# Prompt's value tiles, attention from the third plain tile, operand loads beside plain tiles, ordered taps, fp32 branches

## The chip, the cores and the metric

One core of one Trainium2 chip runs the whole program in one launch. The metric is device time in microseconds (us); the time before is the median of three runs.

## The reference, cut to what matters

One encoder layer is applied with the same weights to a prompt group (512 tokens) and a sample group (1024 tokens). The model width is 1024 and the FFN width 2816, all in fp32.

```python
def token_mixer(h, ...):                       # h = rms_norm(x, norm1_g)
    z = h @ w_in                               # 1024 -> 6400 columns
    br_a = conformer_conv(z[..., OFF_A:OFF_B]) # GLU, depthwise conv of 31 taps, LayerNorm, SiLU, @ w_out_a
    br_b = multiscale_pool(z[..., OFF_B:OFF_C])
    br_c = short_gated_conv(z[..., OFF_C:OFF_D])
    q, k, v = jnp.split(z[..., OFF_D:OFF_G], 3, axis=-1)
    br_d = neighbourhood_attention(q, k, v, rpb) @ w_out_d
    gates = jax.nn.sigmoid(z[..., OFF_G:].reshape(b, t, 4, 1024) + b_gate)
    merged = gates[:, :, 0] * br_a + gates[:, :, 1] * br_b + gates[:, :, 2] * br_c + gates[:, :, 3] * br_d
    return merged @ w_o
...
x = x + token_mixer(rms_norm(x, norm1_g), ...)
x = x + conv_glu_ffn(rms_norm(x, norm2_g), w_up, ffn_conv_w, w_down)
return rms_norm(x, final_g)
```

## The kernel before

The 1536 tokens stand in the columns, in three chunks of 512 (chunk 0 is the prompt, 1 and 2 the sample); the 1024 features are eight blocks `k` of 128 partitions. An fp32 product is made of three matmuls on a high and a low part of each operand (`mm3`, lines 121 to 125: high by high, high by low, low by high). `split` (line 113) makes the two parts: a copy on ScalarE and a subtraction on VectorE. All transfers are issued from one queue, SyncE's (`SP.dma_start`). The kernel is written in a framework that places semaphores itself and fixes each engine's order of instructions ahead of the run: a planner takes, among the instructions that its model holds ready, the one written first. `tc.high_priority()` lets a block go ahead of that; `keep_in_program_order` pins an instruction behind the one that was written just before it on its engine.

The stages that the change touches, in order:

- **Row sums, queries, keys, values** (lines 320 to 509). For chunk 0 the four tiles `z0` (two of queries, two of keys) are made of un-normalized x (`raw0`), for chunks 1 and 2 of normalized h. `stats` (384) squares x on ScalarE and adds on GpSimd and VectorE; `scale` (395) turns the sums into a factor per token with 16 one-column matmuls and some twelve small VectorE steps (`rms_scale`, 138), and writes it on a diagonal `dg`; `spread` (154) sends it over all partitions by one matmul; `norm` (401) multiplies x by it and splits. `qk_out` (406) writes q and k to DRAM. `value_tile` (468) makes the values of 128 tokens with 24 matmuls of 256 columns and writes them by 8 small transfers; it runs for chunks 1, 2, 0, all three on normalized h, after the queries and keys. Beside chunk 1's value tiles chunk 0 is normalized (line 505), beside chunk 2's `operands` (487) writes the pair operands T1 to T4 to DRAM.
- **Plain tiles and attention** (517 to 759). Twelve tiles of 128 output features over three chunks (`ftile`, 24 matmuls for each chunk) feed the conformer, pooling and short-conv branches. Attention has 24 steps; `start` (630) loads q and k of a pair of heads, and `pump(STEPS)` writes 0.7 of a step for each chunk of a plain tile. Attention of the first pair of heads is started ahead of the first plain tile. Branch results are split and both parts go to DRAM (`branch`, `spill`).
- **Gate stage** (764 to 922). The 32 gate tiles are made in 16 pairs; chunks 1 and 2 by a scheme of seven products `y`, `wz`, `xz` on combined operands and combined weights (`PairWeights`, 230), chunk 0 by two plain tiles. `side` (789) is a second stream of work, written between the products by `tick`: 62 taps of the 31-tap conv (2 on ScalarE, 60 on VectorE, line 804) and then the LayerNorm and SiLU. With TAPS = 6, six of its pieces are written for each pair.
- **Merge** (931 to 956). Gates are read back (`g`, 1 MB each), the branches are projected and multiplied by the gates. `load_bs` (855) reads the branch parts from DRAM.

After that come the projection with `w_o` and the FFN, which the change leaves as they are.

## Time and profile before

| | |
|---|---|
| median of 3 runs | 2310.15 us (2308.76 to 2310.45) |
| profiled execution | 2310.91 us, its span 2309.1 us |
| TensorE busy | 2213.5 us, 96% of the span |
| VectorE, ScalarE, GpSimd busy | 1332.6, 771.9, 612.3 us |
| mean granted TensorE clock | 0.975 of full speed |
| DMA | 269.63 MB, mean 117 GB/s |

Busy times are those of one execution under the hardware profiler. A granted clock of 1.00 stands for 2.4 GHz and 0.50 for 1.2 GHz. A row of a window gives its bounds, its length, then busy us and instructions of TensorE's matmuls, its weight loads, VectorE, ScalarE and GpSimd, then the granted clock, the DMA share and GB/s. In the views a line is that of the helper that records the instruction, so the tile names tell the stages apart: `zt` and `z0` queries and keys, `zv` values, `z` plain tiles, `s`, `tp`, `o` attention, `yg`, `wg`, `xg`, `ppg` gates, `y` merge.

### The profile page before, as it was taken

Reading aid. Unit: us, or ns where it says so; the run is one execution under the profiler, and the core shown is the slowest. Engines: PE = TensorE matmul, PEld = TensorE weight load, DVE = VectorE, ACT = ScalarE, POOL = GpSimd, SP = SyncE. Lnnn points to the kernel's source line nnn. Section 1 sums busy time; section 2 is a strip of 40 time slices with the busy share of each in tenths; the row PEclk is TensorE's granted clock in tenths of the full one; section 3 lists DMA queues with packets and bytes.
Section 4 is the critical chain, followed back from the end, with each engine's and each line's share of the span. In section 5 each row is a group of like instructions: output and inputs, shape, how many; then the busy total and the mean of one; then the engine's idle time right before and its main releaser. Section 6 shows DMA issues by size and latency. Waiting matters only on the chain.

```text
span 2309.1 us, 27008 instructions
## 1 busy us (share of the span) xinstructions
PE 2213.5 (96%) x9898; PEld 1797.7 (78%) x9898; DVE 1332.6 (58%) x1946; ACT 771.9 (33%) x1322; POOL 612.3 (27%) x695
## 2 busy tenths in 40 slices
PE   6896999999999999989999999999999999999997
PEld 4794767767788878868787788888888888888886
DVE  4742374588932234167618898788887775441414
ACT  4322544433233335200313443333333333321112
POOL 2111322223211112044224444444444440000001
PEclk8897999999999999999999999999999999999998
DMA  5265251363132223776342321111111114532231
GB/s 208 88 226 173 92 176 67 105 226 119 58 122 86 80 85 141 256 282 226 129 128 93 136 74 64 64 56 63 65 60 64 64 60 153 189 107 70 69 97 51
DMA packets 121205, 269.63 MB, mean 117 GB/s; under 512 B 13808, under 2 KB 24560, under 8 KB 118000
## 3 DMA queue, kind: packets, MB, share of 16 engines
q1 hardware_dynamic: 121072, 267.90, 34.3%
q8 instruction: 78, 1.28, 0.2%
q14 instruction: 55, 0.45, 0.1%
HBM read 173.73 MB, written 94.12 MB: 116 GB/s over the span
## 4 chain that ended last, share of the span: by engine, by line
PE 48%; DVE 2%; issue 0%; POOL 0%; DMA 0%; ACT 0%; POOLq 0%; SPq 0%; DVEq 0%; ACTq 0%
PE yp L124 5%; PE yp L125 5%; PE yp L123 5%; PE ppu L123 3%; PE ppu L125 3%; PE ppu L124 3%; PE o L124 2%; PE o L125 2%; PE o L123 2%; PE p3T L124 1%; PE p3T L123 1%; PE p3T L125 1%; PE p2T L125 1%; PE p2T L124 1%; PE p1T L124 1%; PE p1T L125 1%
## 5 line engine op out<-in xcount | busy, mean ns | idle before, releaser
L123 PE MATMUL yp<-fs,wdhi 128*128 128x512 f32 x480 | 187.0, 391 | 0.0
L124 PE MATMUL yp<-fs,wdhi 128*128 128x512 f32 x480 | 186.9, 389 | 0.0
L125 PE MATMUL yp<-fs,wdlo 128*128 128x512 f32 x480 | 186.8, 389 | 0.0
L1140 POOL TENSOR_TENSOR u<-u,u 128x512 f32<-128x512 f32 x63 | 97.3, 1544 | 194.5 <-DVE u L1133 131.2
L115 DVE TENSOR_TENSOR fs<-fr,fs 128x512 fp32r<-128x512 f32 x63 | 43.5, 690 | 181.5 <-ACT fs L114 181.5
L804 DVE SCALAR_TENSOR_TENSOR acc<-glu,pt,acc 128x1552 f32<-128x1552 f32 x60 | 122.2, 2036 | 12.9 <-ACT acc L802 11.9
L123 PE MATMUL z<-hh,wh_i 128*128 128x512 f32 x288 | 118.4, 411 | 0.2 <-ACT wh_i L114 0.2
L124 PE MATMUL z<-hl,wh_i 128*128 128x512 f32 x288 | 116.4, 404 | 0.0
L125 PE MATMUL z<-hh,wl_i 128*128 128x512 f32 x288 | 115.7, 402 | 0.0
L114 ACT CAST fs<-fr 128x512 fp32r<-128x512 f32 x63 | 39.1, 621 | 198.6 <-DMA fr<-f_d 100.8
L123 PEld LDWEIGHTS yp<-fs,wdhi 128*128 128x128 f32 x480 | 90.1, 188 | 19.4 <-issue 0.5
L124 PEld LDWEIGHTS yp<-fs,wdhi 128*128 128x128 f32 x480 | 90.1, 188 | 19.4 <-issue 0.5
L592 POOL TENSOR_TENSOR bm<-R,pt 128x384 f32<-128x384 f32 (+1 forms) x48 | 44.7, 936 | 228.0 <-DVE mx L599 164.1
L1233 POOL TENSOR_TENSOR x<-x,rs 128x256 f32<-128x256 f32 x11 | 7.6, 730 | 367.0 <-DVE acc L1221 363.3
L125 PEld LDWEIGHTS yp<-fs,wdlo 128*128 128x128 f32 x480 | 90.1, 188 | 18.6
L1133 DVE SCALAR_TENSOR_TENSOR u<-c,pt,u 128x512 f32<-128x512 f32 x88 | 100.4, 1179 | 0.0
L1132 DVE SCALAR_TENSOR_TENSOR u<-c,pt,u 128x512 f32<-128x512 f32 x88 | 86.9, 1025 | 0.0
L123 PE MATMUL y<-bh,wh_wo 128*128 128x512 f32 x192 | 75.6, 394 | 10.0 <-DVE g L942 10.0
L1139 ACT ACTIVATE u<-u 128x512 f32<-128x512 f32 x66 | 41.8, 633 | 112.4 <-DVE u L1133 112.3
L942 DVE TENSOR_TENSOR g<-y,g 128x512 f32<-128x512 f32 x96 | 62.1, 682 | 27.1 <-DMA g<-gate_d 18.8
L124 PE MATMUL o<-ml,wh_o 128*128 128x512 f32 x192 | 75.1, 391 | 1.4 <-DVE ml L115 1.4
L124 PE MATMUL y<-bl,wh_wo 128*128 128x512 f32 x192 | 75.4, 393 | 0.0
(497 smaller groups left out, 6420.9 us busy)
## 6 DMA issues: line engine op xcount, KB each, us to landing
g<-gate_d SPq DMA_DIRECT2D x24, 1024.0 KB, 5.3
wr_u<-in_w_up SPq DMA_DIRECT2D x44, 512.0 KB, 3.5
f_d<-u SPq DMA_DIRECT2D x66, 256.0 KB, 2.0
fr<-f_d SPq DMA_DIRECT2D x66, 256.0 KB, 2.6
wr_g<-in_w_in SPq DMA_DIRECT2D x32, 512.0 KB, 4.0
wdr<-in_w_dn SPq DMA_DIRECT2D x23, 512.0 KB, 3.6
gate_d<-gp SPq DMA_DIRECT2D x32, 256.0 KB, 4.1
x<-in_xT SPq DMA_DIRECT2D x24, 256.0 KB, 5.7
```

What stands on the lines that cost most here:

```text
L114: S.copy(hi, src)
L115: V.tensor_tensor(lo, src, hi.bitcast(F32), ALU.subtract)
L123: PE.matmul(ps, w[0][:, ws], x[0], start=first, stop=False, **kw)
L124: PE.matmul(ps, w[0][:, ws], x[1], start=False, stop=False, **kw)
L125: PE.matmul(ps, w[1][:, ws], x[0], start=False, stop=last, **kw)
L592: G.tensor_tensor(bmv, rv, cm[:, None, :].broadcast_to([P, nk, 32]), ALU.add)
L804: V.scalar_tensor_tensor(a, g, w, a, ALU.mult, ALU.add)
L942: V.tensor_tensor(g[:, i], z, g[:, i], ALU.mult)
L1132: V.scalar_tensor_tensor(b, r[:, 0:C], pc("fc", f * 3), b, ALU.mult, ALU.add)
L1133: V.scalar_tensor_tensor(b, r[:, 2 : C + 2], pc("fc", f * 3 + 2), b, ALU.mult, ALU.add)
L1139: S.activation(ug, ug, AF.Silu)
L1140: (V if j == NJ - 1 else G).tensor_tensor(uv, uv, ug, ALU.mult)
```

## The change

- Order of loads at the start: the remaining query weights, half of chunk 1 of x, the remaining key weights, the parameters, the rest of chunk 1, the value weights, chunk 2. Chunk 1 is squared first, then chunk 0.
- The prompt's four value tiles are made of un-normalized x right after the four `z0` tiles, and scaled by the row factor as they leave PSUM. The first two `norm` of chunk 1 and `qk_out` of chunk 0 are written between them, all `norm` steps with high priority. Chunk 0 of x is loaded a second time beside chunk 2's value tiles and normalized there, each first step pinned.
- Plain tiles take the chunks in the order 1, 2, 0. Two plain tiles are written ahead of attention; STEPS is 0.95. Attention's buffers lie in a group of their own, which is closed once its last step is written and two plain tiles are left. The pair operands are loaded from then on.
- Each VectorE tap is pinned in program order; five pieces of `side` are written for each gate pair.
- Branch results go to DRAM as one fp32 tile and are split after they are read back.
- Pools are placed on two sides of the memory; the tiles for big rows in the plain stage fall from 8 to 3.

```diff
-STEPS = 0.7
-TAPS = 6
+STEPS = 0.95
+TAPS = 5
...
-    bs_d = {(i, k, c): dram(f"bs_d{i}{k}{c}", [2, P, C]) for i in range(4) for k in range(2) for c in range(NC)}
+    bs_d = {(i, k, c): dram(f"bs_d{i}{k}{c}", [P, C]) for i in range(4) for k in range(2) for c in range(NC)}
...
-        def spill(i, k, c, hi, lo):
-            for t, m in ((hi, 0), (lo, 1)):
-                SP.dma_start(bs_d[i, k, c][m], t.bitcast(F32))
+        pairs = [(gates[2 * n], gates[2 * n + 1]) for n in range(16)]
+
+        def keep(ins):
+            return tc.keep_in_program_order(ins)
+
+        tp = None
+
+        def tt(name, dt=F32):
+            return tp.tile([P, C], dt, tag="t", name=name)
...
-            SP.dma_start(pt, par[:, NG:])
-            for k in range(KT):
-                load_x(k, 1)
+            def square(k, c):
+                q = tt(f"sq0_{c}{k}")
+                S.activation(q, x[k, c], AF.Square)
+                if k in (0, 4):
+                    sq[c, k] = q
+                else:
+                    a = sq[c, k & 4]
+                    (V if c == 1 and k > 4 else G).tensor_tensor(a, a, q, ALU.add)
+
+            more_w(0, 13, HD**-0.5)
+            for k in range(4):
+                load_x(k, 1)
+            more_w(1, 15, None)
+            SP.dma_start(pt, par[:, NG:])
+            for k in range(4, KT):
+                load_x(k, 1)
+            for k in range(KT):
+                square(k, 1)
+            vw = [[tt(f"vw{m}{a}", F32R) for a in range(4)] for m in "hl"]
+            for t in range(2):
+                raw = wp.tile([P, DM], F32, tag="wraw", name=f"wr_v{t}")
+                SP.dma_start(raw, w_in[16 + t])
+                for a in range(4):
+                    hi, lo = (vw[m][a].rearrange("p (k t d) -> p k t d", k=2, t=2)[:, :, t, :] for m in range(2))
+                    split(hi, lo, raw[:, a * 256 : (a + 1) * 256].rearrange("p (k d) -> p k d", k=2))
+            for k in range(KT):
+                square(k, 0)
...
             def scale(c):
                 ps = ztile(f"rb0_{c}")
                 dg = tt(f"dg0_{c}")
-                rms_scale(dg, ps, stat[c], DM)
-                stat[c] = dg, ps
+                y = rms_scale(dg, ps, [sq[c, 0], sq[c, 4]], DM)
+                stat[c] = dg, ps, y
 
...
                 z0[n] = ztile(f"zt0{n}")
                 for k in range(KT):
                     w, ws = quad_w(n, k)
                     mm3(z0[n], w, ws, raw0[k], k == 0, k == KT - 1)
-                    if n == 1 and k == 2:
+                    if n == 3 and k == 5:
+                        scale(1)
+                    if n == 3 and k == 6:
                         scale(0)
-                    if n == 1 and k == KT - 1:
-                        spread(*stat[0])
-                        rbp = tt("rbp")
-                        S.copy(rbp, stat[0][1])
-                    if n == 3 and k == 3:
-                        scale(1)
...
-                    split(hi, lo, raw[:, a * 256 : (a + 1) * 256].rearrange("p (k d) -> p k d", k=2))
-
-            def value_tile(c, b):
+
+            def value_tile(c, b, hc, ys=None):
                 z = ztile(f"zv{c}{b}")[:, :256]
                 for k in range(KT):
-                    xh, xl = (y[:, cols(b)] for y in h[c][k])
+                    xh, xl = (y[:, cols(b)] for y in hc[k])
...
-                split(oo[:, :, 0], oo[:, :, 1], z.rearrange("t (p d) -> t p d", p=2))
+                zz = z.rearrange("t (p d) -> t p d", p=2)
+                if ys is None:
+                    split(oo[:, :, 0], oo[:, :, 1], zz)
+                else:
+                    split_scaled(oo[:, :, 0], oo[:, :, 1], zz, ys[:, b : b + 1])
...
+            for b in range(4):
+                value_tile(0, b, raw0, stat[0][2])
+                if b == 1:
+                    spread(*stat[1][:2])
+                    spread(*stat[0][:2])
+                    rbp = tt("rbp")
+                    S.copy(rbp, stat[0][1])
+                if b > 1:
+                    with tc.high_priority():
+                        norm(b - 2, 1)
+                    for n in (2 * b - 4, 2 * b - 3):
+                        qk_out(*QUAD[n], 0, z0[n])
+            for c in (1, 2):
+                zz = [ztile(f"zt{c}{n}") for n in range(4)]
+                for k in range(KT):
+                    if c == 2 or k > 1:
+                        with tc.high_priority():
+                            norm(k, c)
+                    for n in range(4):
+                        w, ws = quad_w(n, k)
+                        mm3(zz[n], w, ws, h[c][k], k == 0, k == KT - 1)
+                    if c == 1:
+                        square(k, 2)
+                    if c == 1 and k == 7:
+                        scale(2)
+                if c == 1:
+                    spread(*stat[2][:2])
+                for n in range(4):
+                    qk_out(*QUAD[n], c, zz[n])
...
-            for c in (1, 2, 0):
+            for c in (1, 2):
                 for b in range(4):
-                    value_tile(c, b)
+                    value_tile(c, b, h[c])
                     if c == 1:
+                        operands(b)
+                    else:
                         for k in (2 * b, 2 * b + 1):
-                            V.scalar_tensor_tensor(x[k, 0], x[k, 0], pc("g1", k), rbp, ALU.mult, ALU.mult)
+                            load_x(k, 0)
+                            keep(V.scalar_tensor_tensor(x[k, 0], x[k, 0], pc("g1", k), rbp, ALU.mult, ALU.mult))
                             h[0][k] = pr[k] = hl(f"hh{k}_0"), hl(f"hl{k}_0")
                             split(*h[0][k], x[k, 0])
-                    if c == 2:
-                        operands(b)
-
...
-                gop = pool(p1, "gop", 7)
-                ap = pool(p1, "ap", 2)
-                kp = pool(p1, "kp", 2)
+                bigp = pool(p1, "bigp", 3, side="right")
+                gop = pool(p1, "gop", 5, side="right")
+                att = p1.enter_context(ExitStack())
+                ap = pool(att, "ap", 2)
+                kp = pool(att, "kp", 2)
+                qp = pool(att, "qp", 4)
...
-                            branch(3, p, qc, ot[:, ch(qc)])
+                            SP.dma_start(bs_d[3, p, qc], ot)
 
                     def start():
                         for n in "qk":
                             for m in "hl":
-                                pl_, tag = (bigp, "big") if n == "q" else (kp, "k")
-                                t[n + m] = pl_.tile([P, PADW], F32R, tag=tag, name=f"{n}{m}{p}")
-                                SP.dma_start(t[n + m][:, :T].bitcast(F32), qk_d[n, p, m])
+                                t[n + m] = (qp if n == "q" else kp).tile([P, T], F32R, tag=n, name=f"{n}{m}{p}")
+                                SP.dma_start(t[n + m].bitcast(F32), qk_d[n, p, m])
...
+                            o = go(f"ob{i}{c}")
+                            S.activation(o, m, AF.Copy, scale=pc("ps", i))
+                            SP.dma_start(bs_d[1, i, c], o)
...
-                        branch(2, i, c, o)
+                        SP.dma_start(bs_d[2, i, c], o)
...
+                def operand_loads():
+                    nonlocal tp
+                    att.close()
+                    tp = pool(tstack, "tpb", TPN)
+                    for n in ("T2", "T3", "T1", "T4"):
+                        for k in range(4):
+                            ops[n, k] = tt(f"{n}gh{k}", F32R), tt(f"{n}gl{k}", F32R)
+                            for m in range(2):
+                                SP.dma_start(ops[n, k][m].bitcast(F32), t_d[n, k][m])
+
+                cb = [conv_branch(i) for i in range(2)]
+                sh = [short_branch(i) for i in range(2)]
+                cb[0][0]()
+                cb[0][1]()
                 attention_pair(0)
-                conv_branch(0)
-                conv_branch(1)
+                cb[1][0]()
                 pool_branch(0)
+                cb[1][1]()
                 pool_branch(1)
                 attention_pair(1)
-                sh = [short_branch(i) for i in range(2)]
                 sh[0][0]()
+                sh[0][1]()
                 sh[1][0]()
-                sh[0][1]()
+                sh[0][2]()
                 sh[1][1]()
+                sh[1][2]()
 
...
+                wg = PairWeights("g", lambda n: tuple(w_in[gate_idx(*g)] for g in pairs[n]), lambda name: tt(name))
-                    for c in range(NC):
+                    left -= 1
+                    for c in (1, 2, 0):
...
                         pump(STEPS)
-                while bg:
-                    bg.pop(0)()
+                        if left < 3 and not bg and tp is None:
+                            operand_loads()
+                assert tp is not None
...
-            tp = pool(phb, "tpb", TPN)
-            go1 = pool(phb, "gob", 8)
+            cvp = pool(phb, "cvp", 2, side="right")
+            go1 = pool(phb, "gob", 8, side="right")
...
-            for n in ("T2", "T3", "T1", "T4"):
-                for k in range(4):
-                    ops[n, k] = tt(f"{n}gh{k}", F32R), tt(f"{n}gl{k}", F32R)
-                    for m in range(2):
-                        SP.dma_start(ops[n, k][m].bitcast(F32), t_d[n, k][m])
...
-                            V.scalar_tensor_tensor(a, g, w, a, ALU.mult, ALU.add)
+                            keep(V.scalar_tensor_tensor(a, g, w, a, ALU.mult, ALU.add))
...
-                        hi, lo = go(f"ch{i}{c}", F32R), go(f"cl{i}{c}", F32R)
-                        split(hi, lo, a)
-                        spill(0, i, c, hi, lo)
+                        SP.dma_start(bs_d[0, i, c], a)
...
+                        t = go(f"bs{i}{k}{c}")
+                        SP.dma_start(t, bs_d[i, k, c])
                         bs[i, k, c] = hl(f"bh{i}{k}{c}"), hl(f"bl{i}{k}{c}")
-                        for m in range(2):
-                            SP.dma_start(bs[i, k, c][m].bitcast(F32), bs_d[i, k, c][m])
+                        split(*bs[i, k, c], t)
```

## Rows read from the trace of the kernel before

**Rows 1.** Windows (start:end, length, busy by engine with counts, clock, DMA), the opening.
```profile
0.00:46.00 46.00, 34.88 (x130) 26.47 (x130) 16.77 (x38) 21.40 (x37) 11.62 (x13) 0.89 0.62 215
46.00:61.10 15.10, 2.08 (x2) 0.50 (x2) 15.10 (x28) 7.34 (x13) 6.89 (x5) 0.54 0.37 139
61.10:71.20 10.10, 9.51 (x30) 8.17 (x31) 5.74 (x14) 2.48 (x4) 2.75 (x2) 0.50 0.00 0
88.80:116.00 27.20, 25.36 (x115) 20.55 (x114) 25.97 (x39) 14.27 (x25) 5.25 (x4) 1.00 0.51 193
118.00:148.00 30.00, 30.00 (x252) 30.00 (x252) 21.08 (x31) 11.17 (x25) 6.10 (x4) 1.00 0.58 179
```
**Rows 2.** Windows: ahead of attention, and the plain stage behind it.
```profile
182.10:214.00 31.90, 12.69 (x38) 9.22 (x39) 7.31 (x23) 8.06 (x19) 4.10 (x9) 0.58 0.72 251
214.00:447.00 233.00, 229.03 (x1106) 169.96 (x1106) 118.41 (x300) 105.73 (x236) 70.72 (x83) 1.00 0.30 104
```
**Rows 3.** Windows: four stretches of the gate stage, then the start of the merge.
```profile
484.90:498.00 13.10, 8.60 (x24) 6.30 (x24) 11.97 (x8) 2.52 (x5) 5.14 (x2) 0.74 0.53 204
556.00:580.00 24.00, 19.59 (x75) 15.62 (x74) 22.06 (x16) 8.49 (x15) 9.32 (x4) 0.86 0.30 99
601.00:613.00 12.00, 9.62 (x36) 7.45 (x35) 11.93 (x10) 3.58 (x7) 4.89 (x2) 0.86 0.37 133
641.00:971.20 330.20, 330.20 (x1453) 270.39 (x1452) 94.80 (x167) 130.86 (x201) 58.76 (x43) 1.00 0.36 120
971.20:998.00 26.80, 16.79 (x66) 13.43 (x65) 6.94 (x11) 0.69 (x1) 3.62 (x3) 0.81 0.93 343
```
**Rows 4.** Waits of TensorE (waiter, releaser: us in total, times, longest us).
```profile
PE s L583 <- DMA kh<-kh_d: 12.2, 1, 12.2
PE yg L123 <- ACT ga L868: 8.0, 3, 4.4
```
**Rows 5.** Timeline of TensorE, 5 to 61 us (start, us, instruction, [idle before <- releaser]).
```profile
5.28 0.79 PE L123 MATMUL zt<-rh,wh_q 128*128 128x512 f32 x1 [5.28 <-ACT rh L118]
...
43.49 1.62 PE L142 MATMUL rb<-ones,sq 128*128 128x1 f32 x14
...
53.53 2.08 PE L155 MATMUL rb<-dg,ones 128*128 128x512 f32 x2 [7.62 <-DVE dg L147]
```
**Rows 6.** Timeline of VectorE, 54 to 62 us.
```profile
53.99 5.76 DVE L505 SCALAR_TENSOR_TENSOR x<-x,pg,rbp 128x512 f32<-128x512 f32 x4
59.68 2.05 DVE L402 SCALAR_TENSOR_TENSOR x<-x,pg,rb 128x512 f32<-128x512 f32 x3
```
**Rows 7.** Timeline of SyncE's queue, 125 to 188 us.
```profile
125.88 25.44 SPq L482 DMA_DIRECT2D vt_d<-vs  x48
...
187.28 0.32 SPq L635 DMA_DIRECT2D kh<-kh_d  x1
```
**Rows 8.** Timeline of VectorE, 471 to 506 us: taps (L804) and what stands behind them.
```profile
471.19 16.79 DVE L804 SCALAR_TENSOR_TENSOR acc<-glu,pt,acc 128x1552 f32<-128x1552 f32 x9
487.90 0.68 DVE L906 TENSOR_TENSOR gs<-yg,gs 128x512 f32<-128x512 f32 x1
...
503.08 2.86 DVE L804 SCALAR_TENSOR_TENSOR acc<-glu,pt,acc 128x1552 f32<-128x1552 f32 x1
```
**Rows 9.** Timeline of GpSimd, 502 to 505 and 558 to 562 us.
```profile
502.71 1.61 POOL L252 TENSOR_TENSOR Sg<-wr_g,wr_g 128x512 f32<-128x512 f32 x1 [6.60 <-DVE Sg1s L115]
...
558.55 2.75 POOL L252 TENSOR_TENSOR Sg<-wr_g,wr_g 128x512 f32<-128x512 f32 x1 [10.43 <-DVE Sg1s L115]
```
**Rows 10.** The taps by their line: duration ns min/median/max, first and last start us.
```profile
L804 DVE SCALAR_TENSOR_TENSOR acc<-glu,pt,acc x60: 1820/1835/2869, 466.4 to 637.3; 128x1552 f32<-128x1552 f32 x60
```
**Rows 11.** Timeline of VectorE in a late pair, 908 to 928 us.
```profile
908.83 0.69 DVE L913 TENSOR_TENSOR gu<-wg,gu 128x512 f32<-128x512 f32 x1 [2.84 <-PE wg L125]
...
927.88 0.69 DVE L883 TENSOR_TENSOR ga<-xg,ga 128x512 f32<-128x512 f32 x1 [4.04 <-PE xg L125]
```
**Rows 12.** Timeline of SyncE's queue, 983 to 1001 us.
```profile
983.73 16.77 SPq L937 DMA_DIRECT2D g<-gate_d  x5
```

92 lines of the change are left out of this document (26 added, 66 removed).

## The prediction

> **What bounds the kernel now.** TensorE is busy for 2213.5 of 2309.1 us, so only its idle time and its slow clock can be won. I read the waits of TensorE first, then windows around each, and in a window I count as lost the idle time plus the busy time times what the clock lacks to 1.00. The reader is to see four places. In the opening, four windows lose 15.0, 14.0, 5.3 and 1.8 us [rows 1], for instance 46.00:61.10: 15.10 - 2.08 idle and 0.46 x 2.08 for the clock. Ahead of attention 19.2 us idle and 0.42 x 12.69, 24.5 us [rows 2]. In the gate stage 6.7, 7.2 and 3.7 us; at the merge 10.0 and 0.19 x 16.79, 13.2 us [rows 3]. The four are 36.1, 24.5, 17.6 and 13.2 us, together 91.4. Elsewhere TensorE is full: 229.03 of 233.00 us in the plain stage [rows 2], 330.20 of 330.20 in the late gate stage [rows 3].
>
> Each has a cause in the rows. In the opening TensorE waits 7.62 us for the diagonal `dg` of chunk 1 [rows 5], and then VectorE, busy for 15.10 of 15.10 us [rows 1], puts four normalizations of chunk 0, which nobody needs yet, ahead of the first `norm` of chunk 1 [rows 6]. Ahead of attention it waits 12.2 us for `kh` [rows 4]; that load was issued at 187.28, because SyncE's queue was still issuing value writes, 48 of them in 25.44 us, 0.53 us each [rows 7]. In the gate stage nine taps stand in a row for 16.79 us, and the add that gives a PSUM bank back comes behind them [rows 8]; the 8.0 us for `ga` [rows 4] lie in such places. At the merge the 1 MB gate loads are issued from 983.73 on [rows 12], behind 48 transfers of branch parts, with the DMA 0.93 busy over the window [rows 3].
>
> **The change part by part.**
>
> Prompt's values beside the row sums. No matmul is added. The four tiles are 96 matmuls of 30.00/252 = 0.119 us [rows 1], 11.4 us of work that needs no row sum, put where TensorE now waits. By that place two factor computations (14 of the one-column matmuls take 1.62 us each time [rows 5]) and the spreads are there as before. Squaring chunk 1 first and pinning chunk 0's normalization takes the eight steps of line 505 out of the way: four of them cost 5.76 us [rows 6]. Of the 36.1 us the first 5.3 are the first load [rows 5], which stays, as does some slow clock behind it, say 2. Against the rest stands VectorE: into the stretch where it is already full come 16 splits of the value weights and four of the tiles, of 256 columns, half of the 0.68 us of a 512-column add [rows 8], 6.8 us; out of it go eight of 1.44 us (5.76/4), 11.5. The prompt tiles hold PSUM banks until the row factor is there. I take 5 us for both. Gain 36.1 - 7.3 - 5 = 24; bounds 12 (half of the wait stays with VectorE) and 28. Loading chunk 0 of x again adds 8 transfers on SyncE's queue and no work for TensorE.
>
> Attention from the third plain tile. Before attention SyncE issues 96 value writes, 32 operand writes and the q and k of two chunks. A third of the value writes moves into the opening, so at 0.53 us about 17 us leave the queue ahead of `kh`; the second reads of x add 8 x 0.53 = 4. Two plain tiles are 144 matmuls of 330.20/1453 = 0.227 us [rows 3], 32.7 us, and lie between the last value tile and attention as they did. So relative to TensorE the load comes some 13 us earlier at most, against a wait of 12.2 us and the further steps that then run at half clock. If the opening shrinks by 24 us the queue must follow: its operand writes start with the normalized chunk 2, which comes earlier by the same amount. I keep 5 us of the 24.5, gain 19; bounds 0 and 24.5. The third plain tile's weights stand in the same queue and are late if it is late.
>
> Density of attention. 24 steps go over 30 chunk-tiles in place of 36. No instruction is added. In the plain stage VectorE is busy for 118.41 of 233.00 us and ScalarE for 105.73 [rows 2]; at 36/30 that is 61% and 54%, so the plain matmuls go on covering it. I take a loss of 2 us, for bounds of 0 and 8 (twice the 3.97 us that are idle there now [rows 2]).
>
> Operand loads and taps. 32 loads of T1 to T4 move into the last two plain tiles, 33 us of TensorE; at 0.53 us their issue takes 17. What hides them is that attention is done by then; if its buffers come free later, the first pair waits as now, when `T2` is read while it lands. The taps lose the freedom to run in a row: five of 1.835 us [rows 10] for a pair of 132 matmuls x 0.227 = 30 us. They stand behind the last weight split of the next pair, so they still come as five in a row, 9.2 us; the next add that frees a bank is due 927.88 - 908.83 = 19.0 us after the one before that burst [rows 11]. So the burst fits, and 17.6 us of loss become 0 to 2: gain 16, bounds 8 and 17.6. Queued behind the pinned taps on VectorE are the adds of `xg` and `yg` and the weight splits of the pair after the next.
>
> Here the trace shows taps of 1.82 to 2.87 us [rows 10], and the one of 2.86 us runs at 503.08 while a GpSimd add of weights runs from 502.71 for 1.61 us [rows 8, 9]. The Trainium skill, page "SBUF — State Buffer", section "Summary: rules for kernel authors", says that a VectorE instruction with two SBUF inputs and a GpSimd instruction that reads SBUF block each other for the whole of the one that came first. By that rule a tap could lose a whole GpSimd add; the trace agrees that the two hold each other up, but by the rows a tap lost 1.05 us at most. By the rows the sum stays, by the rule it is the third rival's, 2257.
>
> Branches in fp32. 48 writes of 256 KB become 24, and 48 reads become 24: 24 x 0.262 MB at 343 GB/s [rows 3] are 18 us of DMA less between the last pair and the first gate tile, more than the 10.0 us idle. The 24 splits that the plain stage loses come back here, 24 x 0.69 = 17 us on VectorE, which is busy for 6.94 of the 26.80 us [rows 3]. But with five pieces for a pair instead of six the LayerNorm now ends in the last pair, and its results for chunks 1 and 2 are written, read and split after it; chunk 1 is needed 2 x 24 x 0.227 = 11 us into the merge. Gain 10, bounds 0 and 13.2.
>
> **Sum.** 24 + 19 - 2 + 16 + 10 = 67 us. The profiled execution took 2310.9 us (its span 2309.1, 1.8 around it), 0.8 above the median of 2310.15. 2310.9 - 67 = 2243.9, so I say 2244 us.
>
> **The rivals.** First, SyncE's queue still sets the start of attention: the planner puts the loads behind all writes, or the second reads of x hold up chunk 0 of the first plain tile. That this already happens by 12.2 us speaks for it, the 17 us taken out against it. The 19 us are not won: 2263. This is also the case in which attention doesn't start where the title says. Second, the opening is VectorE's: it is full for 15.10 of 15.10 us [rows 1] and most of its work stays. Then 12 of 24 us are won: 2256. Third, taps and GpSimd's adds hold each other up. Four adds for a pair take up to 2.75 us [rows 9]; if taps lose all of that, five take 9.2 + 11 = 20 us against the 19.0 us that the next add leaves, 1 us lost in each of 13 pairs: 2257. Fourth, on the slow side: the pinned taps themselves become the wait. They come right when a pair ends, and if each of 13 pairs lost what 556:580 lost, 7.2 us [rows 3], that is 94 us where I count 1.6, so 2244 + 92 = 2336. It decides from (67 + 1.6)/13 = 5.3 us a pair. For it speaks that taps in a row did hold the bank's add [rows 8]; against it that five take half of nine, and that the 19 us are free.
>
> **How the numbers follow.** Forecast 0.59, first rival 0.15, second 0.12, third 0.06, fourth 0.06; 0.02 for a mild fourth that eats just the gain. A measurement of this kernel can tell 0.2%, 4.6 us, from no change: faster 0.92, same 0.02, slower 0.06. The low end is nearly all of the 91.4 us but the first load's 7.3 won, 2310.9 - 84 = 2227, and a little more, 2222; the high end takes in the first three rivals and some of two at once, 2270.
>
> **What would show it.** Right: no window of the opening after 20 us with TensorE under 85% and the last value tile some 24 us earlier, where the window to 148.00 is still full of them [rows 1]; the first `s` matmul behind two plain tiles with a wait under 5 us; the first gate pair without a wait for T2 or `gs`; taps in groups of five, none nine in a row, spread over 13 pairs; 24 reads of branches and the first gate load issued before TensorE has filled its PSUM banks. Wrong: `kh` still over 8 us late, a wait for `hh` or `dg` of over 5 us, TensorE waiting for `ga` or `gs` once a pair, or a wait at the merge for the branch of the conv.

## The result and the profile after

The changed kernel takes 2275.38 us (median of four runs, 2273.6 to 2279.49) against 2309.76 of the kernel before beside it: a ratio of 0.9854 (95% interval 0.9837 to 0.9871), 34 us faster. The forecast was 2244, with 2222 to 2270 as its range: the sign is right, half of the 67 us is missing, and the time lies outside the range. The profiled execution took 2275.41 us, its span 2273.6.

I cut both spans at four instructions of TensorE: the first `z` matmul (plain tiles), the first `yg` (gate stage), the first `y` (merge) and the first `o` (projection).

| stage | before | after | change | forecast |
|---|---|---|---|---|
| opening, to the first `z` | 149.2 | 133.4 | -15.8 | -24 |
| plain tiles and attention, to `yg` | 308.2 | 304.0 | -4.2 | -17 (-19, +2) |
| gate stage, to `y` | 513.8 | 492.0 | -21.8 | -16 |
| merge, to `o` | 142.7 | 149.5 | +6.8 | -10 |
| the rest | 1195.2 | 1194.7 | -0.5 | 0 |
| span | 2309.1 | 2273.6 | -35.5 | -67 |

Three stages missed: opening by 8, attention by 13, merge by 17; the gate stage gave 6 more. The four stages of after as windows (columns as in [rows 1]; TensorE's busy time stands second, behind the length):

```profile
0.00:133.40 133.40, 118.23 (x630) 100.61 (x631) 90.75 (x151) 59.33 (x109) 36.12 (x27) 0.94 0.56 195
133.40:437.40 304.00, 286.32 (x1342) 212.81 (x1342) 135.06 (x342) 123.87 (x272) 82.97 (x94) 0.97 0.43 143
437.40:929.40 492.00, 490.03 (x2156) 402.29 (x2155) 265.62 (x290) 190.86 (x295) 119.20 (x71) 1.00 0.32 103
929.40:1078.90 149.50, 133.28 (x577) 109.83 (x576) 104.82 (x147) 26.31 (x37) 61.27 (x46) 0.94 0.66 234
```

The gate stage is full: 490.03 of 492.00 us at a clock of 1.00, where it had three holes [rows 3]. The merge still has 16.2 us of idle time, the plain stage 17.7. TensorE's waits in the whole of after (waiter, releaser: us in total, times, longest):

```profile
PE y L123 <- DVE g L975: 16.2, 1, 16.2
PE z L123 <- ACT hh L114: 11.8, 3, 10.1
PE rb L156 <- DVE dg L147: 6.8, 3, 3.8
...
PE rb L142 <- POOL sq L385: 3.3, 1, 3.3
```

Against [rows 4]: the waits for `kh` (12.2 us) and `ga` (8.0) are gone. New are 11.8 us for `hh`, the split of the second reads of x. The wait of the first product with a gate is not new, but it has grown from 10.0 to 16.2 us; before, it read

```profile
PE y L123 <- DVE g L942: 10.0, 1, 10.0
```

The windows of after around the four waits:

```profile
30.00:40.00 10.00, 6.71 (x36) 6.14 (x36) 8.56 (x13) 4.04 (x8) 8.32 (x6) 0.68 0.19 59
...
80.00:90.00 10.00, 6.00 (x16) 4.04 (x17) 8.09 (x17) 2.47 (x4) 1.28 (x1) 0.57 0.28 107
145.00:160.00 15.00, 5.42 (x12) 3.78 (x13) 4.32 (x7) 1.85 (x3) 0.00 (x0) 0.66 0.79 246
930.00:958.00 28.00, 11.78 (x49) 9.45 (x49) 13.70 (x21) 12.55 (x19) 0.68 (x1) 0.77 0.81 283
```

What stands behind the second wait is in SyncE's queue (start, us, transfers), the counterpart of [rows 7]:

```profile
123.78 12.20 SPq L473 DMA_DIRECT2D vt_d<-vs  x24
...
150.36 0.87 SPq L338 DMA_DIRECT2D x<-in_xT  x2
151.32 3.65 SPq L473 DMA_DIRECT2D vt_d<-vs  x8
155.01 0.92 SPq L338 DMA_DIRECT2D x<-in_xT  x2
...
181.55 0.42 SPq L656 DMA_DIRECT2D kl<-kl_d  x1
```

The second reads of x go out two at a time from 150.36 on, each pair behind eight value writes; TensorE had stood since 144.5. The last load of keys is issued at 181.55; before, even `kh`, the one ahead of it, went out at 187.28. And behind the first wait, at the merge, SyncE's queue (now as in [rows 12]) and VectorE:

```profile
931.81 0.38 SPq L874 DMA_DIRECT2D bs_d<-acc  x1
932.71 0.32 SPq L818 DMA_DIRECT2D gate_d<-gr  x1
933.08 12.02 SPq L890 DMA_DIRECT2D bs<-bs_d  x16
950.70 1.27 SPq L970 DMA_DIRECT2D g<-gate_d  x3
```

```profile
948.71 1.97 DVE L115 TENSOR_TENSOR bl<-bs,bh 128x512 fp32r<-128x512 f32 x3 [0.34 <-ACT bh L114]
955.81 3.15 DVE L975 TENSOR_TENSOR g<-y,g 128x512 f32<-128x512 f32 x5 [5.14 <-DMA g<-gate_d]
```

LayerNorm's last branch is written at 931.81, two us after the last product; then 16 reads take 12.0 us, VectorE splits until 950.68, and the first gate load is issued at 950.70 (983.73 was 12.5 us into the merge before; this is 21.3).

### The profile page after: what moved, and what is told of

It reads as the page before. It is cut to its first block, busy times and chain, and to the rows that moved or that the text cites. A ratio compares the mean times of both kernels' runs of the same rounds, so it can differ in the third digit from the quotient of the medians.

```text
span 2273.6 us, 26886 instructions
## 1 busy us (share of the span) xinstructions
PE 2199.9 (97%) x9898; PEld 1789.9 (79%) x9898; DVE 1351.8 (59%) x1946; ACT 781.3 (34%) x1328; POOL 632.4 (28%) x695
## 4 chain that ended last, share of the span: by engine, by line
PE 49%; DVE 2%; issue 0%; POOL 0%; POOLq 0%; ACT 0%; DVEq 0%; ACTq 0%
PE yp L124 5%; PE yp L123 5%; PE yp L125 5%; PE ppu L125 3%; PE ppu L123 3%; PE ppu L124 3%; PE o L124 2%; PE o L123 2%; PE o L125 2%; PE p3T L125 1%; PE p3T L124 1%; PE p3T L123 1%; PE p1T L124 1%; PE p1T L125 1%; PE p1T L123 1%; PE p22T L125 1%
## 5 line engine op out<-in xcount | busy, mean ns | idle before, releaser
L123 PE MATMUL z<-hh,wh_i 128*128 128x512 f32 x288 | 120.1, 418 | 11.8 <-ACT hh L114 11.8
L123 PE MATMUL y<-bh,wh_wo 128*128 128x512 f32 x192 | 75.8, 395 | 16.2 <-DVE g L975 16.2
L614 POOL TENSOR_TENSOR bm<-R,pt 128x384 f32<-128x384 f32 (+1 forms) x48 | 47.3, 990 | 151.5 <-DVE mx L621 124.4
L253 POOL TENSOR_TENSOR Sg<-wr_g,wr_g 128x512 f32<-128x512 f32 x16 | 22.0, 1376 | 217.9 <-DVE Sg1s L115 217.9
L123 PEld LDWEIGHTS z<-hh,wh_i 128*128 128x128 f32 x288 | 55.3, 192 | 28.9 <-ACT hh L114 13.7
```

What stands on the lines that cost most here:

```text
L123: PE.matmul(ps, w[0][:, ws], x[0], start=first, stop=False, **kw)
L253: G.tensor_tensor(t, x, y, op)
L614: G.tensor_tensor(bmv, rv, cm[:, None, :].broadcast_to([P, nk, 32]), ALU.add)
```

## The experiments

Ratios are to the kernel before; 0.9854 is the changed kernel's. Unless said otherwise an experiment is the changed kernel with the edit shown, and stages are cut as above.

### Attention's start

**Values on ScalarE's queue.**

```diff
-                        SP.dma_start(
+                        S.dma_start(
                             vt_d[j, c * 8 + b * 2 + r],
```

> The changed kernel, with the 96 value writes (vt_d, eight per tile) issued on ScalarE's queue instead of SyncE's. Theory A (SyncE's queue is what kept the attention and the second reads of x late): in the changed kernel PE waits 10.06 us for hh at 144.3 and the clock is 0.81 and 0.72 afterwards, while the second reads of x were issued from 150.36 on between value writes of 3.65 us a group. Off that queue they go out earlier by some 10 us: the wait for hh falls below 3 us, the first score comes 5 us or more earlier than 191.2, the plain stage and attention shrink by 10 to 18 us, and the time falls to about 2260. Theory B (the buffers of the second reads come free late, or the operands' own writes hold the queue): the reads go out when they did, the wait for hh stays at 8 us or more, and the time stays within 4 us of the changed kernel's 2275.4. Theory C: ScalarE, which issues in its own order, stands still behind values not yet split, its copies come late, and the time is longer by 5 us or more.

2281.37 us (0.9874, 0.9858 to 0.9891): theory C. The second reads went out earlier, from 141.9 on, but ScalarE issues in its own order: 24 value writes keep its queue for 21.95 us (0.91 us each), and its copies for the last four value tiles come behind them.

```profile
133.49 21.95 ACTq L473 DMA_DIRECT2D vt_d<-vs  x24
155.49 1.20 ACT L114 CAST vs<-zv 128x256 fp32r<-128x256 f32 x4 [21.93 <-DMA wr_i<-in_w_in]
```

The opening is 140.1 us (6.7 more; 2 to 5 us more also appear in runs that leave the opening as it is, see the last section), and behind it TensorE waited as long as in the changed kernel, for another thing, the split of a value tile (`vs`):

```profile
PE z L123 <- DVE vs L115: 11.6, 1, 11.6
```

**Second reads first.**

```diff
-                            load_x(k, 0)
+                            with tc.high_priority():
+                                load_x(k, 0)
```

> The changed kernel, with the eight second reads of x raised ahead of the value and operand writes in SyncE's queue, nothing else. Theory A1 (their place behind value writes is what costs, as the first rival of the prediction had it): the wait for hh of 10.06 us at 144.3 goes to under 2 us, the clock of 0.81 and 0.72 after it to 0.95 or more, and the time falls by 11 to 18 us, to 2258 to 2265, though the first score stays near 191, since kh and kl still leave behind the value writes. Theory B (their buffers come free only when the operands of chunks 1 and 2 are done, so that an earlier place makes SyncE itself wait): the reads land no earlier than 152, what is queued behind them comes later, and the time is the same or longer by up to 10 us.

2273.08 us (0.9835, 0.9820 to 0.9849), which can't be told from the changed kernel. The profile is half of theory A1: no wait for `hh`, plain stage and attention 297.0 instead of 304.0, but not 11 us less. What is late next is the weights of the third plain tile, whose load stands behind 32 value writes of 0.52 us each:

```profile
152.11 16.52 SPq L473 DMA_DIRECT2D vt_d<-vs  x32
168.68 0.43 SPq L202 DMA_DIRECT2D wr_i<-in_w_in  x1
```

```profile
PE z L123 <- ACT wh_i L114: 6.2, 1, 6.2
```

**Values of chunks 1 and 2 on GpSimd's queue, second reads first.**

```diff
-                        SP.dma_start(
+                        (G if c else SP).dma_start(
                             vt_d[j, c * 8 + b * 2 + r],
...
+                            with tc.high_priority():
+                                load_x(k, 0)
```

> The changed kernel with the second reads of x raised as in the run on them, and the 64 value writes of chunks 1 and 2 issued on GpSimd's queue, which has little else from 100 to 185 us. There TensorE waited 6.2 us for the third tile's weights, whose load was issued at 168.68 behind 32 value writes of 16.5 us on SyncE's queue. Theory A (the number of transfers that SyncE issues sets attention's start): the weights' load and q and k go out by 160, no wait over 2 us remains ahead of attention, and the time is 7 to 14 us under that run's 2273. Rival D (the transfers themselves, not their issue: the DMA is 0.65 to 0.98 busy there): q, k and the weights land no earlier, and the time stays within 3 us. Rival G: GpSimd issues a transfer more slowly than SyncE's 0.52 us, vv waits for the values, and the time is longer.

2259.58 us (0.9781, 0.9766 to 0.9795): theory A. Plain stage and attention fall to 285.2 us, 23.0 less than before the change where the forecast had 17. The weights leave at 147.9, the keys by 153, the first score comes at 174.5 instead of 191.2, and TensorE has no gap from 145 to 185:

```profile
145.00:160.00 15.00, 15.00 (x68) 12.43 (x67) 3.17 (x4) 4.54 (x6) 9.09 (x19) 1.00 0.99 331
160.00:185.00 25.00, 25.00 (x121) 19.99 (x120) 6.00 (x20) 8.64 (x15) 14.03 (x29) 1.00 0.81 320
```

With SyncE issuing everything the DMA moved 246 GB/s in 145 to 160, at a share of 0.79; now it moves 331, at 0.99. It was the issuing queue, not the transfers, that set the pace there.

### The merge

**Six taps a step, as before the change.**

```diff
-TAPS = 5
+TAPS = 6
```

> The changed kernel with six taps between products in place of five, so that convolution and LayerNorm are done some two pairs before the merge instead of beside its start. Theory L (the late LayerNorm holds up the reads of the branches, which start at 933.08, 1.3 us after its last write): the 16.23 us in which PE stands at 940 to 956.65 shrink to 8 us or less and the time falls by 6 to 12 us. Theory R (the 16 reads of 12 us behind the last gate's write and the splits, and the gate's reads behind these, set it): the wait stays at 13 to 16 us and the time within 3 us of the changed kernel's.

2287.84 us (0.9898, 0.9884 to 0.9913): 12 us longer, foreseen by neither theory. The merge does get shorter, by 4.6 us to 144.9, so LayerNorm's late end is a part of it; but the gate stage grows by 11.2 to 503.2. Another 4.8 us of the profiled execution lie in the opening (138.2), which the edit leaves as it is. LayerNorm's first sums `mu`, written right behind the read of the stored convolution, stand in TensorE's queue until that read has landed:

```profile
PE mu L850 <- DMA accn<-acc_d: 11.7, 1, 11.7
PE y L123 <- DVE g L975: 11.5, 1, 11.5
```

**Gate buffers elsewhere.**

```diff
-                    gp = pool(p2a, "gp", 3, side="right")
+                    gp = pool(p2a, "gp", 3)
```

> The changed kernel with the merge's gate buffers in another part of the memory than the gate stage's own buffers, so that the first gate read needn't wait for the last split of a branch (950.68, the read goes out at 950.70, after 5 us without transfers). Theory G: the gate reads go out at about 945.5, right behind the branch reads, PE's wait for g falls by about 5 us, from 16.2 to 11, and the time by 4 to 7 us. Rival: what is late next, the splits of the branches that PE reads (to 950.68), holds PE as long; the time stays within 2 us.

2274.31 us (0.9845, 0.9825 to 0.9865), not told from the changed kernel. In the profile the gate read goes out 0.3 us behind the branch reads and the merge is 2.5 us shorter (147.0): the rival in the main, the splits on VectorE are late next.

**Six taps, four steps ahead of LayerNorm, chunk 1's branches before the last two products, gate buffers elsewhere** (with the two edits above).

```diff
                 SP.dma_start(acc[0][:, LO:HI], acc_d)
-                yield
+                for _ in range(4):
+                    yield
...
+                if end:
+                    for _ in step:
+                        pass
+                    load_bs(1)
                 product(wz, w["22"], "T4", False, True)
...
-            load_bs(1)
             load_bs(2)
```

> The changed kernel with six taps between products, four steps between the read of the stored sums and LayerNorm, the merge's gate buffers elsewhere, and the reads and splits of the branches of chunk 1 ahead of the last pair's last two products. If the merge's start is set by 16 reads (12.0 us) and 16 splits on VectorE (0.69 us each) that stand in the queues ahead of the first gate read and the first product with g, half of both is now hidden: the wait for g falls from 16.2 to 8 us or less, the wait for the stored sums (11.7 us with six taps alone) goes, the gate stage stays at 492 to 494 us and the time falls by 7 to 11 us. Rival: the early reads and splits hold up the last pair's gate writes or splits, or six taps hold up the products' sums, and the gate stage grows by as much as the merge gains.

2266.57 us (0.9819, 0.9802 to 0.9837), as expected. The wait for `g` is 5.4 us, the gate stage 490.2, and the merge

```profile
927.20:1065.30 138.10, 132.66 (x577) 109.37 (x576) 102.39 (x144) 21.42 (x31) 61.31 (x46) 0.98 0.67 237
```

is 11.4 us shorter than after and 4.6 shorter than before. How the 11.4 us divide among the four edits stays open.

**Branches in two halves again.** `bs_d` has its two halves back; each branch is split where it is made, written twice and read straight into its operands.

```diff
-                            SP.dma_start(bs_d[3, p, qc], ot)
+                            spill(go, 3, p, qc, ot)
...
-                        t = go(f"bs{i}{k}{c}")
-                        SP.dma_start(t, bs_d[i, k, c])
-                        split(*bs[i, k, c], t)
+                        for m in range(2):
+                            SP.dma_start(bs[i, k, c][m].bitcast(F32), bs_d[i, k, c][m])
```

> The changed kernel with the branches written and read as two halves (fp32r high and low), split where they are made, as in the kernel before: the last part of the change undone alone. The prediction has this part worth 10 us, so that undoing it costs 10 and gives 2285. The merge of the changed kernel, 149.5 us against 142.7 before, speaks for the rival: the reads in fp32 and their splits ahead of the merge cost what the saved writes give; undone, the merge is 3 to 8 us shorter, attention and gate stage together 3 to 8 us longer by the splits there, and the time stays within 4 us of the changed kernel's 2275.

2284.87 us (0.9893, 0.9878 to 0.9908): the prediction's price of 10 was nearly right in size (9.5 us by the medians, 7.4 by the two profiled executions), my rival wrong in the merge. But only 2.9 us of it lie in the merge (152.4); 5.0 lie in plain stage and attention, 309.0 us, where VectorE has 17 instructions and 12.9 us more. So the branches aren't what made the merge longer.

### The gate stage

**Taps unpinned.**

```diff
-                            keep(V.scalar_tensor_tensor(a, g, w, a, ALU.mult, ALU.add))
+                            V.scalar_tensor_tensor(a, g, w, a, ALU.mult, ALU.add)
```

> The changed kernel with the taps left free again for the planner to move, five pieces for a pair, all else as changed. In the changed kernel the gate stage is 492.0 us and TensorE is busy for 490.03 of them; before, it was 513.8. Theory T (pinning is what keeps the taps from standing in a row ahead of the adds that give PSUM banks back): waits for ga and gs return in the first third of the stage, 8 to 14 us together with slow clock behind them, and the time is 2283 to 2292. Rival N (five pieces instead of six and the operands loaded ahead do it alone): the gate stage stays within 3 us of 492 and the time within 4 us of 2275.

2287.40 us (0.9902, 0.9887 to 0.9916): theory T. The gate stage is 10.6 us longer (502.6), with waits of 3.9 us for `gs`, 2.9 for `ga` and 2.6 for `gu`.

**The kernel before, with pinned taps and five pieces alone.**

```diff
-TAPS = 6
+TAPS = 5
...
-                            V.scalar_tensor_tensor(a, g, w, a, ALU.mult, ALU.add)
+                            tc.keep_in_program_order(V.scalar_tensor_tensor(a, g, w, a, ALU.mult, ALU.add))
```

> The kernel before with only the taps pinned in program order and five pieces for a pair instead of six; opening, attention, operand loads and branches as before. If pinning carries the gate stage, its waits for ga (8.0 us) and gs (3.2 us) go, the first pair's T2 loss (6.7 us with its clock) stays, and the gate stage falls from 513.8 to about 500; at the merge, LayerNorm's late branches then cost 3 to 8 us more than the 10.0 us waited before. Sum: 4 to 10 us faster than before, 2300 to 2306. If the operand loads carry it, the gate stage stays over 508 and the time is that of before or, by the later LayerNorm, up to 6 us longer.

2303.52 us (0.9974, 0.9964 to 0.9984), as expected, though its merge loses more than the 3 to 8 us that it was given. Its gate stage and merge:

```profile
456.10:956.40 500.30, 494.90 (x2157) 403.94 (x2156) 264.22 (x289) 189.79 (x295) 121.37 (x70) 0.99 0.36 123
956.40:1109.90 153.50, 133.71 (x578) 110.14 (x577) 95.87 (x133) 17.67 (x23) 61.33 (x46) 0.93 0.70 253
```

The gate stage gains 13.5 us and the merge loses 10.8, its wait 19.8 instead of 10.0: this run has the old branches, buffers and reads. What moved is LayerNorm's end: its last branch part is written at 960.08, 3.7 us into the merge, where before it was written at 903.5, 68 us ahead of it. The remaining 8.3 us of the gate stage (500.3 to 492.0) come from the rest of the change, the operand loads among it.

### The opening

**Chunk 2's factor two steps earlier.**

```diff
-                    if c == 1:
-                        square(k, 2)
-                    if c == 1 and k == 7:
+                    if c == 1 and k < 4:
+                        square(2 * k, 2)
+                        square(2 * k + 1, 2)
+                    if c == 1 and k == 5:
                         scale(2)
```

> The changed kernel with chunk 2's squares written two to a step and its scaling factor after the sixth step of chunk 1's loop instead of after the last. In the changed kernel PE waits 3.83 us for dg at 82.5 and 1.5 us for hh behind it, is busy 6.00 of 10 us in 80 to 90, and the clock there is 0.57, though the sums of chunk 2 were ready at about 61. Theory P (the place in program order): both waits go, the clock of 80 to 90 rises to 0.9 or more, the opening is shorter by 5 to 8 us and so is the time. Rival V (VectorE, busy 10.00 of 10 us in 50 to 60, can't do the factor, the eight norms of 5.36 us and the splits any sooner): PE waits for hh instead, and the time stays within 2 us of the changed kernel's.

2274.05 us (0.9849, 0.9827 to 0.9871): no gain that can be told; its four executions lie between 2269.57 and 2281.02 us, so one of a few us could hide. The wait for `dg` in that place is gone; TensorE then waits 2.7 us for a normalized x, behind eight scalings that take 5.36 us in a row. This is rival V.

**Chunk 0's sums on VectorE.**

```diff
-                    (V if c == 1 and k > 4 else G).tensor_tensor(a, a, q, ALU.add)
+                    (V if c == 0 or c == 1 and k > 4 else G).tensor_tensor(a, a, q, ALU.add)
```

> The changed kernel with the six square sums of chunk 0 on VectorE instead of GpSimd. In the changed kernel VectorE's steps on 128x4 take 1.22 to 1.24 us from 32.48 to 39.6, beside GpSimd's six adds of 1.44 us each (30.99 to 39.62), and 0.16 to 0.17 us afterwards. Theory L (the two engines hold each other up): with no GpSimd add there the steps take 0.16 us throughout, chunk 1's factor, now 9 us from 31.4 to 40.6, takes 6 us or less with the adds between its steps, PE's wait of 3.29 us for the sums falls below 2 us, and the time falls by 2 to 5 us. Rival V (VectorE's own load is what makes the factor late, the second rival of the prediction): six adds of 0.68 us are 4.1 us more for VectorE, the factor comes no earlier, and the time stays or rises by up to 4 us.

2277.01 us (0.9858, 0.9844 to 0.9873). The mechanism is theory L, the time is not, and TensorE's wait for the sums is 3.9 us, not below 2. In the changed kernel (first fence GpSimd, second VectorE)

```profile
30.99 8.63 POOL L385 TENSOR_TENSOR sq<-sq,sq 128x512 f32<-128x512 f32 x6 [5.14 <-ACT sq L380]
```

```profile
32.48 1.23 DVE L131 TENSOR_SCALAR rs_y<-rs_v 128x4 int32<-128x4 int32 x1
33.95 1.22 DVE L133 SCALAR_TENSOR_TENSOR rs_t<-rs_y 128x4 f32<-128x4 f32 x1
...
39.88 0.16 DVE L135 SCALAR_TENSOR_TENSOR rs_y<-rs_t,rs_y 128x4 f32<-128x4 f32 x1
...
46.37 1.28 DVE L147 TENSOR_TENSOR dg<-pt,rs_y 128x512 f32<-128x512 f32 x2
48.27 5.36 DVE L421 SCALAR_TENSOR_TENSOR x<-x,pg,rb 128x512 f32<-128x512 f32 x8 [0.62 <-PE rb L156]
```

each small step starts 1.47 us behind the one before, about one GpSimd add (8.63/6 = 1.44). The Trainium skill, page "SBUF — State Buffer", section "Summary: rules for kernel authors", says that a VectorE instruction with two SBUF inputs, or in a mode that takes both ports, and a GpSimd instruction that reads SBUF can't run together: the second to issue is blocked until the first is through. The trace agrees here: 1.22 to 1.24 us against 0.16. In this run, without those adds, the steps take 0.16 us throughout, and chunk 1's factor is done at 37.7 instead of 40.6. But its diagonal still starts at 46.08: in VectorE's fixed order it stands behind chunk 0's factor and a value split.

```profile
37.56 0.16 DVE L135 SCALAR_TENSOR_TENSOR rs_y<-rs_t,rs_y 128x4 f32<-128x4 f32 x1
...
46.08 1.28 DVE L147 TENSOR_TENSOR dg<-pt,rs_y 128x512 f32<-128x512 f32 x2
```

**Chunk 0's row sums behind two value tiles** (and its square sums on VectorE as above).

```diff
-                    if n == 3 and k == 6:
-                        scale(0)
...
+                if b == 0:
+                    z2 = [value_mm(0, a, raw0) for a in range(2)]
+                    scale(0)
```

> The changed kernel with chunk 0's row sums on TensorE behind two value tiles instead of ahead of the first, and chunk 0's square sums on VectorE. With the sums on VectorE alone TensorE waited 3.91 us for sq and then 4.3 for dg, though the factor of chunk 1 was done 3 us earlier. Theory Q (TensorE stands in its own queue at sums that aren't ready, and the clock of 30 to 50 us falls behind that): the wait for sq falls below 1 us, the spread comes at 44 instead of 48, the clock of 30 to 50 rises, and opening and time are 4 to 8 us shorter. Rival: the wait only moves to dg, whose factor is late for VectorE's splits; the opening stays within 2 us.

2275.90 us (0.9852, 0.9835 to 0.9868): the rival. The wait for `sq` is 0.3 us, and 3.4 us come up at the third value tile, whose bank waits for a split that needs chunk 0's factor.

**The whole chain in another order.** The diagonal of chunk 1 pinned ahead of chunk 0's factor, its spread behind two value tiles, chunk 2's factor at `k == 4` and its spread at `k == 6`, the parameters loaded ahead of the remaining weights, sums and tiles as in the last run, and the scalings two ahead of the splits:

```diff
+                    scaled(0)
+                    keep(scaled(1))
+                    for k in range(KT):
+                        h[c][k] = hl(f"hh{k}_{c}"), hl(f"hl{k}_{c}")
+                        S.copy(h[c][k][0], x[k, c])
+                        keep(V.tensor_tensor(h[c][k][1], x[k, c], h[c][k][0].bitcast(F32), ALU.subtract))
+                        if k + 2 < KT:
+                            keep(scaled(k + 2))
```

> The changed kernel with only VectorE's and TensorE's order in the opening altered: the diagonal dg of chunk 1 ahead of chunk 0's factor, its spread behind two value tiles, chunk 2's factor and spread inside chunk 1's loop, and in both normalizations the first split behind the second scaling instead of behind the eighth (5.36 us in a row); the parameters are loaded earlier and chunk 0's sums are on VectorE. Single moves gave nothing in three runs, as each only passed the wait on. Theory O (the order of VectorE's instructions, fixed ahead of the run, holds the chain factor, diagonal, spread, scaling, split): the waits for sq, dg and hh fall from 3.3, 3.8 and 1.5 to under 3 together, the windows of 30 to 40 and 80 to 90 us are at least 9 of 10 us busy, and opening and time are 7 to 13 us shorter, near 2265. Rival W (the opening has less work for VectorE-free stretches than it has waiting: transfers of x and sums set it): within 3 us of 2275.

2269.77 us (0.9830, 0.9814 to 0.9846). This is theory O in the opening, which is 124.7 us: 8.7 less than in the changed kernel and 24.5 less than before the change, where the forecast had 24. The waits for `sq`, `dg` and `hh` there fall to 2.0 us together. The time gains 5.6 us by the medians, less than the 7 to 13 expected.

```profile
0.00:124.70 124.70, 115.63 (x630) 98.97 (x631) 88.05 (x157) 58.79 (x109) 27.22 (x21) 0.96 0.58 198
...
30.00:40.00 10.00, 9.01 (x64) 8.88 (x64) 7.46 (x24) 2.86 (x6) 0.00 (x0) 0.83 0.50 167
...
80.00:90.00 10.00, 10.00 (x46) 8.28 (x45) 10.00 (x16) 4.88 (x9) 1.68 (x1) 1.00 0.22 84
```

Of the 8.7 us the next stage gives back 2.1: the wait for `hh` grows to 14.9 us. The order holds in every profile that has it: four openings of 124.3 to 124.9 us, against 133.0 to 140.1 in the changed kernel and the twelve runs of it that lack it.

### Together

**Queue and merge.** The runs with the values on GpSimd's queue and with chunk 1's branches early, put together.

> Two earlier runs put together: second reads first and 64 value writes on GpSimd's queue (2259.6), and six taps with four steps ahead of LayerNorm, chunk 1's branches read ahead of the last products and the gate buffers elsewhere (2266.6). If the two causes are separate their gains add: 15.8 and 8.8 under 2275.4, 2249 to 2253. If the earlier end of attention lets taps or operands collide anew, it is 2256 or more.

2243.44 us (0.9711, 0.9697 to 0.9726). Plain stage and attention 285.7, gate stage 490.3, merge 138.0: each as when it was changed alone, so the causes are separate. The time is 6 us below the expected range, which was added up from medians: by its stages the merge's run had gained 13 us, but in its profiled execution, the fastest of four (2261.45 to 2270.37 us).

**All three.** The same with the opening's order.

> The same with the opening's altered order as well. If theory O holds and the three causes are separate, 7 to 13 us less than the run with two, near 2240; a stage behind the opening that takes them back (the second reads and weights, which then are due earlier) would leave it within 3 us of that run.

2246.47 us (0.9724, 0.9710 to 0.9739): nothing gained. The opening is 124.9, but plain stage and attention 294.1. One order does it: GpSimd's last operand subtraction stands behind 32 value writes, VectorE waits for it, and the second reads go out behind that operand's writes.

```profile
DVE x L533 <- POOL T L532: 8.0, 1, 8.0
```

```profile
PE z L123 <- ACT hh L114: 6.3, 1, 6.3
```

**Operands ahead of the value tiles.**

```diff
+            for b in range(4):
+                operands(b)
             for c in (1, 2):
                 for b in range(4):
                     value_tile(c, b, h[c])
-                    if c == 1:
-                        operands(b)
-                    else:
+                    if c == 2:
```

> The run with all three, with the operands of all four blocks written ahead of the value tiles, so that GpSimd's last subtractions stand ahead of its value writes in GpSimd's order. With all three the opening ended at 124.9 instead of 133.3, but VectorE waited 8.0 us to 133.96 for GpSimd's subtraction T of the last block, which stood behind 32 value writes; the second reads of x went out at 136.9 behind that operand's writes, and TensorE waited 6.3 us for hh. Theory K (this one order takes the opening's 8 us back): the wait for hh falls below 2 us, the plain stage and attention go from 294.1 to 286 to 289, and the time from 2246.5 to 2238 to 2242. Rival D (the transfers are full, 0.95 busy from 125 to 145, and take it back in any order): the wait stays over 4 us or moves to kh or the weights, and the time stays within 3 us of 2246.5.

2233.46 us (0.9668, 0.9652 to 0.9684), the fastest kernel here: theory K, and 4.5 us under its low end.

```profile
123.00:145.00 22.00, 22.00 (x104) 18.45 (x103) 9.25 (x16) 7.11 (x12) 14.79 (x30) 1.00 1.01 330
145.00:160.00 15.00, 15.00 (x68) 12.41 (x67) 4.43 (x5) 2.60 (x3) 8.86 (x18) 1.00 1.01 375
```

Its stages are 124.4, 284.1, 490.3 and 136.9 us; TensorE is full from 123 to 185, with the DMA full as well up to 160.

**Half of the writes on GpSimd's queue.** As with all three, but `G if c == 2 else SP`.

> The run with all three, but with only chunk 2's 32 value writes on GpSimd's queue and chunk 1's on SyncE's, so that GpSimd's subtractions again stand ahead of its writes. Theory K: no wait for hh, and 32 more transfers of 0.52 us on SyncE's queue are 16.6 us, of which part holds up q, k and weights: 2240 to 2250. Rival D: as with all three, within 3 us of 2246.5.

2238.81 us (0.9692, 0.9678 to 0.9706), a little under its range: theory K again, no wait for `hh`, and 5 us dearer than the last run, with a wait of 2.1 us for `kl` and 291.2 us in plain stage and attention.

## Why the prediction was right or wrong

**Bounds.** The four places were the right ones, and nothing outside of them moved (-0.5 us). With the causes named by the runs taken away, in the fastest kernel, they gave 24.8, 24.1, 23.5 and 5.8 us (149.2 to 124.4, 308.2 to 284.1, 513.8 to 490.3, 142.7 to 136.9). So the lost time was there, all but a part of the merge's. What failed is what I let the change leave behind in three of the places: a term too small in the opening, a wait set against the wrong load ahead of attention, and LayerNorm's end, priced at nothing, at the merge.

**Opening, 24 forecast, 15.8 found: residue mis-sized.** "I take 5 us for both" counted VectorE's instructions, in and out, and not their order; 13 us stayed. Chunk 1's diagonal stood behind chunk 0's factor, and the scalings, now with high priority, came eight in a row (48.27 to 53.63) ahead of the first split. The diff also moves chunk 2's factor from the sixth to the eighth step of the loop; I costed that at nothing without saying so, and it shows as 3.8 us for `dg` at 82.5. So TensorE was 67% and 60% busy in 30 to 40 and 80 to 90, where no window was to be under 85%. Another order of the chain, with the parameters loaded earlier, returned 8.7 us. The single moves returned nothing that can be told, and in their profiles each handed the wait to another link; how the 8.7 divide among the links stays open. The second rival, VectorE's load, is not it: the other order gives VectorE six adds more, and its busy time in the opening hardly falls (90.75 to 88.05 us).

**Attention, 19 forecast, about 4 found: the first rival was right and had 0.15.** The wait for `kh` did go, and the steps' density cost little (252.60 of 258.00 us busy from 182 to 440). But I set the second reads of x against `kh` alone, as eight more transfers in a queue; they are needed after 48 matmuls of the first plain tile, before any key, and each pair stands behind eight value writes. The rival named that, and its place, chunk 0 of the first plain tile; the wait is the 10.1 us for `hh`. Behind them came the weights, and then q and k: all from one queue, at 0.46 to 0.53 us a transfer.

**Gate stage, 16 forecast, 21.8 found: right in the mechanism, too small in size.** No wait for `ga` or `gs`. The upper bound of 17.6 came from three windows; over the whole stage before (first line) TensorE was idle for 13.3 us, and its busy time fell by 10.4 us to 490.03 as the clock went from 0.98 to 1.00. The taps do not come five in a row, as I had it, but two, two and one, with splits of weights between them (at 705.39, 709.62 and 715.85 in one pair). They are spread over 373 us, and the second line, of after, answers [rows 10]:

```profile
457.40:971.20 513.80, 500.47 (x2157) 406.41 (x2156) 255.21 (x291) 190.38 (x299) 108.31 (x70) 0.98 0.37 126
...
L837 DVE SCALAR_TENSOR_TENSOR acc<-glu,pt,acc x60: 1821/1834/2937, 487.9 to 861.1; 128x1552 f32<-128x1552 f32 x60
```

Pinning is worth 10.6 us in this stage, by the run without it. The third and fourth rival did not happen: the longest tap takes 2.94 us, and no pair waits for it.

**Merge, 10 forecast as a gain, 6.8 found as a loss: one term priced at nothing.** The branches in fp32 are worth 9.5 us, close to 10, but that is luck: the sum had them as transfers saved at the merge, where 2.9 us of it lie, and the larger part, 5.0, is in plain stage and attention, where the splits no longer run. The prediction said that LayerNorm would now end in the last pair and gave it no price: that is 10.8 us in the kernel before and, by the run with six taps, 4.6 of the merge in the changed one. Six pieces alone would not have been better in the changed kernel (2287.84 us), mainly because of the 11.7 us for the stored convolution; six pieces with a gap behind the start of that read, and half of the branch reads early, are.

**The range.** It was built from one rival at a time and "some of two at once". Here three terms came out near their lower bounds or beneath together: 12, 0 and 0 instead of 24, 19 and 10 would have given 2285.

## What to carry to other kernels

Where an engine waits for a transfer, take the wait away on paper and ask what stands next in the same issuing queue and who needs that first; a queue that is full hands the wait on. A part of the change that ends something later (here LayerNorm) needs a price of its own in the sum. In a chain whose order is fixed ahead of the run, moving one link may show nothing where moving several together shows 8.7 us, so a null result of one link does not clear the chain.

## What the runs showed of the hardware

A transfer of 64 KB from 32 partitions keeps SyncE's queue for 0.46 to 0.53 us, and GpSimd's for 0.49 to 0.57 us, though there it lands later (5.3 us by the median, against 1.7 from SyncE's). 64 of them moved from the one to the other, with the second reads ahead, were worth 16 us, with the same bytes to move. On ScalarE's queue they cost time (0.91 us each for 24 in a row), since that engine's copies stand behind them.

A step of VectorE on 128x4 takes 0.16 us alone and 1.22 to 1.24 us beside GpSimd's adds: in a chain of small dependent steps a step grows to nearly eight times its length, whereas a tap of 1.83 us lost 1.1 at most.

After the stall of 30 to 40 us the granted clock is not the same from run to run where the code is: in 40 to 50 us it was 0.98 in the changed kernel, nearly all of it at 2.4 GHz, but 0.55 with six taps, 0.62 with the gate buffers elsewhere and 0.59 with the taps unpinned, most of it at 1.2 GHz, though the edits of these three lie in the gate stage and the merge, behind 430 us. The opening is 133.4 us in the first and 138.2, 137.0 and 135.9 in the others, and four executions of one kernel lay between 2269.6 and 2281.0. The length of the stall does not decide it: TensorE waited 3.3 us for `sq` ahead of the 0.98, and 3.0 ahead of the 0.59. What does was not found.
